# A hybrid encoder layer on one core: a third PSUM bank for main products, heads' norms by square transposes, and two moved ScalarE/VectorE steps

## The chip, the cores and the metric

The kernel runs on one core of a Trainium2 chip. The metric is the time of one execution on the device in microseconds (us). Five engines work side by side, each on its own instructions in a fixed order, and wait for one another by semaphores: TensorE (PE in the profile, its weight loads PEld), VectorE (DVE), ScalarE (ACT), GpSimd (POOL) and SyncE (SP, which here issues most of the DMAs). TensorE writes its results to PSUM, which has eight banks of 128 x 512 float32 here; the other data lies in SBUF.

## The reference

One layer of an encoder, batch 1, 512 tokens, width 1024, in float32. The part that the change touches is the parallel mixer:

```python
h = _rms_norm(x, norm_mix_pre)
(a_q, a_k, a_v, f_q, f_k, f_v, f_g, c_u, s_x, s_b, s_c) = split(h @ w_in)
# A, differential attention, 4 heads, keys up to the query's chunk of 64:
p = softmax(where(chunk mask, s * scale, -inf))          # two score maps per head
ya = (p[0] - lam * p[1]) @ v
ya = _rms_norm(ya, diff_norm) * (1 - lambda_init)        # over the 128 channels of a head
# B, forgetting attention, 8 heads, causal, bias from a cumulative log forget gate:
yf = softmax(where(causal, s * scale + c_q - c_k, -inf)) @ v
# C, gated convolution of 31 taps with a LayerNorm; D, gated convolution of 3 taps
proj = einsum(stack([ya, yf, yc, ys]), w_branch)
mixed = sum(sigmoid(h @ w_gate + b_gate) * proj) @ w_out
x = x + _rms_norm(mixed, norm_mix_post)
```

Behind it come a cross-attention into 256 memory tokens and a gated MLP with a convolution of 3 taps; the change leaves their code alone.

## The kernel before

Every large product is made of three: each operand is split into a high part (a cast to fp32r, by ScalarE) and a low part (the rest, a subtraction by VectorE), and high x high, high x low and low x high are summed in one PSUM bank (`mm3`). Weights come from HBM as blocks of 512 KB into one of two raw tiles `wr`, are cast to `wh` (L192) and subtracted to `wl` (L193), of which there are four each.

The work is a list of jobs (`run_blocks`). A job's weights are fetched three jobs ahead; its body is usually a product of 128 channels by 512 tokens over eight pieces of 128 rows, so 24 matmuls of 512 columns (`channel_major`), and then its evacuation from PSUM. Beside the jobs run background tasks (`Background`): generators that yield a cost and a waiting time after each step. At each tick, in the middle and at the end of a job, they get credit (0.7 per us of products counted so far, at most 4), and the first two in the queue may take steps as long as credit is left. `drain` runs what is left of a kind at once. This sets the program's order; a scheduler at build time then orders each engine's instructions from it, by dependences, free buffers and its own estimate of times, and `tc.issue_after(x)` places an instruction behind `x` on its engine.

PSUM's eight banks have four names with two banks each: `mm` and `av` (main products; `av` also for the attentions' values), `sc` (scores) and `tr` (transposes). `bank()` without a name takes `mm` and `av` in turn, and only `mm` between `share(False)` and `share(True)`, the two attention stages, where `av` holds values.

The jobs around the change: values of A (`v_jobs`); four pairs of query and key products of A (`qk_jobs`), each of which adds a background task for a head (`a_task`, heads 0 to 3), among them the 12 jobs of gate and branch for the convolution (`gate_blocks(2, "c")`); drain of A's tasks; the values of B (`vf_jobs`, four jobs, whose result takes the one tile `v` that held A's values); four pairs of query and key products of B, each of which adds `f_task` (pairs of heads 0 to 3), among them gate and branch of A; drain of B's tasks; gate and branch of B; then the layer's other parts.

A head of A works in steps, one per 128 queries: scores (two per step, `sc`), exponentials, the difference of the two maps. Heads 0 to 2 ("far") have their probabilities turned to keys-major form by VectorE's square transposes of 32 x 32 blocks (`turn_squares`) and a way through DRAM (`put`, `get`), and split in place two steps later (`split_in_place`); head 3 has them turned on TensorE (`to_keys_major`). Pairs 0 and 1 of B are far, 2 and 3 near. The values of two steps are then summed into an `av` bank (`values`). Head A's end, from L949 on, is its RMS norm: the 128 x 512 result is turned to token-major form by four TensorE transposes, squared (L953), summed (L955), its root taken by GpSimd, scaled (L957), turned back by four more transposes and split into `y["a"]`. The LayerNorm of the convolution (`conv_norm_task`) does the like without TensorE's transposes: VectorE transposes squares of 32 x 32, sums over 32 columns, and one small product with a constant (`over_channels`, L871) adds the four blocks of channels.

`evacuations` holds the newest evacuation that was marked by `main`, `last_weights` the newest weight block's cast and subtraction. In `f_task` the two heads' probabilities are scaled by ScalarE (L1135, `j` = 0) and VectorE (L1133, `j` = 1).

Of the kernel before, what the change touches and what calls it, by code (L numbers as in the profile page):

```python
# [83 lines left out]
def hybrid_layer(ctx: ExitStack, tc: tile.TileContext, a: dict, out: bass.AP):  # L84
# [9 lines left out]

    turn_of = SimpleNamespace(n=0, shared=True)

    def bank(tag=None):
        if tag is None:
            turn_of.n += 1
            tag = "av" if turn_of.shared and turn_of.n % 2 else "mm"  # L100
        return psum.tile([P, 512], F32, tag=tag, name=f"ps_{tag}", bufs=2)

    def share(shared):
        return None, None, lambda: vars(turn_of).update(n=1, shared=shared)

# [755 lines left out]

    def split_in_place(n, pt, local):
        hi, lo = (part_of(x, n, local) for x in pt)
        raw = lo.bitcast(F32)
        with tc.issue_after(evacuations[0]):
            A.copy(hi, raw)
        V.tensor_tensor(lo, raw, hi.bitcast(F32), ALU.subtract)
# [27 lines left out]
    def a_task(h, qk, v):  # L895
# [3 lines left out]
        for step in range(8 if far else 6):  # L899
# [8 lines left out]
            if far:  # L908
                for qt in SPLITS.get(step, ()):
                    split_in_place(qt + 1, pt, qt % 2)  # L910
                    cost += 0.1 + 0.15 * qt
                for qt in GETS.get(step, ()):
                    if qt % 2 == 0:
                        pt = pt_tiles()
                    get(es.pop(qt)[:, 0], qt + 1, pt, qt % 2)
            elif 1 <= step <= 4:
                if step in (1, 3):
                    pt = pt_tiles()
                to_keys_major(es.pop(step - 1)[:, 0], step, pt, (step - 1) % 2)
                cost += 0.1 + 0.15 * step  # L920
# [27 lines left out]
            yield cost, (6.0 if step == 5 else 4.0) if far else 3.5  # L948

        ps = bank("tr")  # L950
        for t in range(NT):
            transpose(ps[:, t * P:(t + 1) * P], e[:, 0, t * P:(t + 1) * P])
        A.activation(e[:, 1], ps, AF.Square, scale=1.0 / math.sqrt(P))  # L953
        ms = m1p.tile([P, NT], F32, tag="ms4", name="ms4", bufs=2)
        V.tensor_reduce(ms, e[:, 1].rearrange("p (t c) -> p t c", t=NT), AX.X, ALU.add)  # L955
        r = rstd_of(m1p, [ms], NT)
        V.tensor_tensor(e[:, 0].rearrange("p (t c) -> p t c", t=NT),  # L957
                        ps.rearrange("p (t c) -> p t c", t=NT),
                        r.unsqueeze(2).to_broadcast([P, NT, P]), ALU.mult)
        yield 1.5, 3.5  # L960
        ps2 = bank("tr")
        for t in range(NT):
            transpose(ps2[:, t * P:(t + 1) * P], e[:, 0, t * P:(t + 1) * P])
        if "a" not in y:
            y["a"] = (y8b(), y8b())
        split(ps2, y["a"][0][:, h], y["a"][1][:, h], half["dn"])
        yield 0.6, 0.0

# [85 lines left out]
    def f_task(p, qk, v):  # L1054
# [19 lines left out]
        for step in range(8 if far else 6):  # L1074
# [14 lines left out]
            if far:  # L1089
# [4 lines left out]
                for qt in GETS.get(step, ()):  # L1094
# [3 lines left out]
                    for j in range(2):  # L1098
                        get(d[:, j], qt + 1, pts[j], qt % 2)
            else:  # L1100
                for qt in {2: (0, 1), 3: (2,), 4: (3,)}.get(step, ()):
                    if qt % 2 == 0:
# [5 lines left out]
            if step < 4:  # L1108
# [22 lines left out]
                for j in range(2):  # L1131
                    if j:
                        V.tensor_scalar(e[:, j, :w], e[:, j, :w], st[:, 6 + j:7 + j], None, ALU.mult)  # L1133
                    else:
                        A.activation(e[:, j, :w], e[:, j, :w], AF.Copy, scale=st[:, 6 + j:7 + j])  # L1135
# [59 lines left out]
    def mixer_jobs():  # L1195
# [20 lines left out]
        yield from vj  # L1216
        yield share(False)
        gc = gate_blocks(2, "c")
# [121 lines left out]
    def last_branch_jobs():  # L1340
# [3 lines left out]
        yield next(gf)  # L1344
        yield share(True)
        yield from gf
# [544 lines left out]
```

## Time and profile before

| | |
|---|---|
| median of 3 runs | 1051.34 us (1051.13 to 1052.14) |
| profiled execution | 1050.01 us, its span 1048.2 us, TensorE's granted clock 0.999 |
| busy, of the span | TensorE 1037.6, weight loads 882.5, VectorE 807.9, ScalarE 508.5, GpSimd 147.5 us |
| first transposes of a head's norm on TensorE | 279.18 us after the start; attention A's queue is empty at about 359 us |
| far pairs of attention B | about 380 to 440 us |

In the profile, a row of a group gives line, engine, operation, the tiles written and read, their shapes and the count; then busy time and the mean length in ns, and the idle time of the engine before them with what ended it. Rows of the timeline give start and length in us. Matmul lengths contain the pipeline's depth, so that two matmuls overlap; how far apart they start tells what one costs. In a row of waits stand the engine, tile and line that waited, what it waited for, the sum in us, the number of times and the longest.

### The profile page before, as it was taken

How to read it: one execution, taken by the hardware profiler on the slowest of the kernel's cores; microseconds unless marked ns; L12 is line 12 of the kernel's file. 1: busy time of each engine (PE TensorE's matmuls, PEld its weight loads, DVE VectorE, ACT ScalarE, POOL GpSimd, SP SyncE). 2: the span in 40 equal slices, each digit the busy share in tenths (PEclk: the TensorE clock that was granted, in tenths of full speed). 3: DMA queues.
4: the chain of work that ended last, by engine and by line, in shares of the span. 5: the costliest groups of instructions: out<-in, count | busy, mean ns of one | idle time of the engine just before them, and what ended most of it. 6: DMA issues, size and time to landing. Idle time of an engine off the chain costs nothing.

```text
span 1048.2 us, 14451 instructions
## 1 busy us (share of the span) xinstructions
PE 1037.6 (99%) x5255; PEld 882.5 (84%) x5255; DVE 807.9 (77%) x1265; ACT 508.5 (49%) x838; POOL 147.5 (14%) x239
## 2 busy tenths in 40 slices
PE   8999999999999999999999999999999999999997
PEld 8888888888888988888888899998888888888886
DVE  7999998677768369876577898776767777667796
ACT  5322222376465356765443666655343333445662
POOL 4001000100000114432101031121112111111001
PEclk9999999999999999999999999999999999999999
DMA  8953333334433246642357734235577666726662
GB/s 272 315 158 90 102 100 101 99 85 122 137 103 110 61 122 186 181 136 81 101 160 265 237 124 137 63 104 189 191 241 225 217 224 218 220 81 183 215 215 81
DMA packets 182141, 163.86 MB, mean 156 GB/s; under 512 B 17151, under 2 KB 154092, under 8 KB 182069
## 3 DMA queue, kind: packets, MB, share of 16 engines
q1 hardware_dynamic: 173027, 131.18, 42.0%
q10 hardware_dynamic: 6482, 23.21, 6.2%
q0 software_dynamic: 2560, 8.54, 2.5%
q8 instruction: 41, 0.67, 0.3%
q14 instruction: 31, 0.25, 0.1%
HBM read 139.43 MB, written 23.48 MB: 155 GB/s over the span
## 4 chain that ended last, share of the span: by engine, by line
PE 98%; DVE 1%; DMA 0%; ACT 0%; issue 0%; POOL 0%; POOLq 0%; DVEq 0%; SPq 0%; ACTq 0%
PE ps_mm L235 53%; PE ps_av L235 30%; PE ps_sc L235 7%; PE ps_tr L235 4%; PE ps_tr L241 2%; PE ps_mm L453 1%; PE ps_av L453 1%; DMA xs<-in_x 0%; ACT e L735 0%; DVE qk L808 0%; PE ps_tr L437 0%; DVE o L1781 0%; PE ps_av L437 0%; ACT qk L806 0%; DVE e L848 0%
## 5 line engine op out<-in xcount | busy, mean ns | idle before, releaser
L192 ACT CAST wh<-wr 128x1024 fp32r<-128x1024 f32 (+1 forms) x140 | 146.6, 1048 | 261.5 <-PE ps_mm L235 158.2
L193 DVE TENSOR_TENSOR wl<-wr,wh 128x1024 fp32r<-128x1024 f32 (+1 forms) x140 | 174.7, 1249 | 85.5 <-ACT wh L192 85.3
L235 PE MATMUL ps_mm<-hth,wh 128*128 128x512 f32 (+1 forms) x616 | 230.5, 381 | 0.4 <-DVE qk L808 0.2
L235 PE MATMUL ps_mm<-hth,wl 128*128 128x512 f32 (+1 forms) x616 | 229.8, 379 | 0.0
L235 PE MATMUL ps_mm<-htl,wh 128*128 128x512 f32 (+1 forms) x616 | 229.7, 379 | 0.0
L235 PEld LDWEIGHTS ps_mm<-hth,wh 128*128 128x128 f32 x616 | 114.1, 188 | 21.9 <-ACT y L158 0.6
L235 PEld LDWEIGHTS ps_mm<-hth,wl 128*128 128x128 f32 x616 | 114.0, 188 | 21.4
L235 PEld LDWEIGHTS ps_mm<-htl,wh 128*128 128x128 f32 x616 | 114.0, 188 | 20.5
L235 PE MATMUL ps_av<-htl,wh 128*128 128x512 f32 (+1 forms) x328 | 122.5, 373 | 0.0
L235 PE MATMUL ps_av<-hth,wh 128*128 128x512 f32 (+1 forms) x328 | 122.4, 373 | 0.0
L235 PE MATMUL ps_av<-hth,wl 128*128 128x512 f32 (+1 forms) x328 | 122.3, 373 | 0.0
L688 DVE SCALAR_TENSOR_TENSOR y<-y,par,y 128x508 f32<-128x508 f32 (+29 forms) x120 | 82.9, 731 | 0.1
L235 PEld LDWEIGHTS ps_av<-hth,wl 128*128 128x128 f32 x328 | 61.7, 188 | 11.0
L235 PEld LDWEIGHTS ps_av<-htl,wh 128*128 128x128 f32 x328 | 61.6, 188 | 10.9
L235 PEld LDWEIGHTS ps_av<-hth,wh 128*128 128x128 f32 x328 | 61.6, 188 | 10.8
L1682 DVE TENSOR_TENSOR wl<-dw,wh 128x1024 fp32r<-128x1024 f32 x32 | 40.1, 1257 | 15.6 <-ACT wh L1681 15.4
L1681 ACT CAST wh<-dw 128x1024 fp32r<-128x1024 f32 x32 | 33.5, 1052 | 22.0 <-PE ps_mm L235 7.4
L1629 ACT ACTIVATE th<-c 128x512 f32<-128x512 f32 x22 | 13.9, 632 | 48.1 <-DVE c L615 48.1
L1116 POOL TENSOR_SCALAR fbias<-ck,cq 128x128 f32<-128x128 f32 (+3 forms) x32 | 27.0, 847 | 70.4 <-DVE st L1122 63.2
L615 DVE SCALAR_TENSOR_TENSOR c<-ps_mm,par,c 128x510 f32<-128x510 f32 (+1 forms) x44 | 32.8, 745 | 0.7
L235 PE MATMUL ps_mm<-y8b,wh 128*128 128x512 f32 x96 | 30.7, 396 | 0.0
L235 PE MATMUL ps_mm<-y,wh 128*128 128x512 f32 x96 | 30.6, 393 | 0.0
(484 smaller groups left out, 2092.4 us busy)
## 6 DMA issues: line engine op xcount, KB each, us to landing
wr<-in_w_up SPq DMA_DIRECT2D x44, 512.0 KB
wr<-in_w_in SPq DMA_DIRECT2D x38, 512.0 KB
wr<-in_w_gate SPq DMA_DIRECT2D x32, 512.0 KB
wp<-in_w_down ACTq DMA_DIRECT2D x22, 512.0 KB
sums<-wp ACTq DMA_DIRECT2D x22, 512.0 KB
dw<-sums SPq DMA_DIRECT2D x44, 256.0 KB
wr<-in_w_branch SPq DMA_DIRECT2D x16, 512.0 KB
wide<-in_w_out SPq DMA_DIRECT2D x12, 512.0 KB
```

Of the source, the lines that this page charges most:

```text
L192: last_weights[:] = [order(A.copy(hi, raw[:, :n])).ins, low.tensor_tensor(lo, raw[:, :n], hi.bitcast(F32), ALU.subtract).ins]
L193: low.tensor_tensor(lo, raw[:, :n], hi.bitcast(F32), ALU.subtract).ins]
L235: steps_of[:] = [PE.matmul(ps, lhs, rhs, start=start, stop=stop).ins]
L241: turns.append(PE.transpose(ps, x, ident[:n, :n]).ins)
L453: keep(PE.matmul(banks[c][:, :S // 2], w[p == 1][:, k, c * P:(c + 1) * P], ht[p == 2][:, i * 4 + k, :S // 2], start=(i, p, k) == (0, 0, 0) ...
L615: ins = V.scalar_tensor_tensor(dst[:, s:], src[:, :S - s], w(k), dst[:, s:], ALU.mult, ALU.add)
L688: ins = V.scalar_tensor_tensor(dst[:, s:], src[:, :S - s], pc("conv_dw", k * 4 + j), dst[:, s:], ALU.mult, ALU.add)
L1116: G.tensor_scalar(bias[:, :w], ck[j][:, :w], -1.0, cq[:, qt, head:head + 1], ALU.mult, ALU.add)
L1629: A.activation(th, c[:, 0], AF.Silu)
L1681: A.copy(hi, x)
L1682: V.tensor_tensor(lo, x, hi.bitcast(F32), ALU.subtract)
```

## The change

- `bank` gets a list of names among which main products take turns. In the attention stages it is `mm`, `mm`, `tr0`: the two `tr` banks become `tr0` and `tr1`, and as long as `tr0` is in the list, transposes take `tr1` alone. From the second step of pair 2 of B on (`step == 2 and p == 2`) the list is `mm`, and transposes have both again; from the last gate stage on it is `mm`, `av` as before.
- The norm of a head of A: one square transpose of the whole result by VectorE, the squares by ScalarE, a sum over 32 columns, `over_channels`, the power by GpSimd on 128 x 16, the scaling, a square transpose back, the split. TensorE's eight transposes per head go, one small product comes. The costs told to `Background` are 2.0, 0.2 and 2.4 with waits of 4.0 and 4.0, in place of 1.5 and 0.6 with a wait of 3.5.
- `split_in_place` takes what its cast is placed behind; in `a_task` it is now `last_weights`. `f_task` still passes nothing and keeps `evacuations`.
- In the far pairs of `f_task` both heads' probabilities are scaled by VectorE.

```diff
--- before.py
+++ after.py
@@ -92,16 +92,22 @@
 
 
 
-    turn_of = SimpleNamespace(n=0, shared=True)
+    turn_of = SimpleNamespace(n=0, tr=0, among=("mm", "av"))
 
     def bank(tag=None):
         if tag is None:
             turn_of.n += 1
-            tag = "av" if turn_of.shared and turn_of.n % 2 else "mm"
-        return psum.tile([P, 512], F32, tag=tag, name=f"ps_{tag}", bufs=2)
-
-    def share(shared):
-        return None, None, lambda: vars(turn_of).update(n=1, shared=shared)
+            tag = turn_of.among[turn_of.n % len(turn_of.among)]
+        elif tag == "tr":
+            turn_of.tr = 1 if "tr0" in turn_of.among else 1 - turn_of.tr
+            tag = f"tr{turn_of.tr}"
+        return psum.tile([P, 512], F32, tag=tag, name=f"ps_{tag}", bufs=1 if tag[:2] == "tr" else 2)
+
+    def share_now(*among):
+        vars(turn_of).update(n=1, among=among)
+
+    def share(*among):
+        return None, None, lambda: share_now(*among)
 
     x_d, mem_d = a["x"][0], a["mem"][0]
     w_in, w_gate, w_out = a["w_in"][0], a["w_gate"][0], a["w_out"][0]
@@ -859,10 +865,10 @@
     def get(d, n, pt, local):
         SP.dma_start(part_of(pt[1], n, local).bitcast(F32), d.rearrange("(a j) (b x) -> (j b) a x", j=32, b=4))
 
-    def split_in_place(n, pt, local):
+    def split_in_place(n, pt, local, after=evacuations):
         hi, lo = (part_of(x, n, local) for x in pt)
         raw = lo.bitcast(F32)
-        with tc.issue_after(evacuations[0]):
+        with tc.issue_after(after[0]):
             A.copy(hi, raw)
         V.tensor_tensor(lo, raw, hi.bitcast(F32), ALU.subtract)
 
@@ -907,7 +913,7 @@
             cost = 0.0
             if far:
                 for qt in SPLITS.get(step, ()):
-                    split_in_place(qt + 1, pt, qt % 2)
+                    split_in_place(qt + 1, pt, qt % 2, last_weights)
                     cost += 0.1 + 0.15 * qt
                 for qt in GETS.get(step, ()):
                     if qt % 2 == 0:
@@ -947,24 +953,22 @@
                 A.copy(e[:, 0], av)
             yield cost, (6.0 if step == 5 else 4.0) if far else 3.5
 
+        V.transpose(e[:, 1], e[:, 0])
+        A.activation(e[:, 0], e[:, 1], AF.Square, scale=1.0 / math.sqrt(P))
+        ms = m1p.tile([P, S // 32], F32, tag="ms4", name="ms4")
+        V.tensor_reduce(ms, by_token(e[:, 0]), AX.X, ALU.add)
+        yield 2.0, 4.0
         ps = bank("tr")
-        for t in range(NT):
-            transpose(ps[:, t * P:(t + 1) * P], e[:, 0, t * P:(t + 1) * P])
-        A.activation(e[:, 1], ps, AF.Square, scale=1.0 / math.sqrt(P))
-        ms = m1p.tile([P, NT], F32, tag="ms4", name="ms4", bufs=2)
-        V.tensor_reduce(ms, e[:, 1].rearrange("p (t c) -> p t c", t=NT), AX.X, ALU.add)
-        r = rstd_of(m1p, [ms], NT)
-        V.tensor_tensor(e[:, 0].rearrange("p (t c) -> p t c", t=NT),
-                        ps.rearrange("p (t c) -> p t c", t=NT),
-                        r.unsqueeze(2).to_broadcast([P, NT, P]), ALU.mult)
-        yield 1.5, 3.5
-        ps2 = bank("tr")
-        for t in range(NT):
-            transpose(ps2[:, t * P:(t + 1) * P], e[:, 0, t * P:(t + 1) * P])
+        over_channels(ps[:, :S // 32], ms)
+        V.tensor_scalar(ms, ps[:, :S // 32], EPS, None, ALU.add)
+        G.tensor_tensor(ms, ms, nhalf[:, :1].to_broadcast([P, S // 32]), ALU.pow)
+        yield 0.2, 4.0
+        V.tensor_tensor(by_token(e[:, 1]), by_token(e[:, 1]), ms.unsqueeze(2).to_broadcast([P, S // 32, 32]), ALU.mult)
+        V.transpose(e[:, 0], e[:, 1])
         if "a" not in y:
             y["a"] = (y8b(), y8b())
-        split(ps2, y["a"][0][:, h], y["a"][1][:, h], half["dn"])
-        yield 0.6, 0.0
+        split(e[:, 0], y["a"][0][:, h], y["a"][1][:, h], half["dn"])
+        yield 2.4, 0.0
 
 
     crows = dram.tile([8, S], F32, name="crows")
@@ -1098,6 +1102,8 @@
                     for j in range(2):
                         get(d[:, j], qt + 1, pts[j], qt % 2)
             else:
+                if step == 2 and p == 2:
+                    share_now("mm")
                 for qt in {2: (0, 1), 3: (2,), 4: (3,)}.get(step, ()):
                     if qt % 2 == 0:
                         pts = [pt_tiles() for _ in range(2)]
@@ -1129,7 +1135,7 @@
                                  scale=HD ** -0.5, accum_out=st[:, 4 + j:5 + j])
                 V.reciprocal(st[:, 6:8], st[:, 4:6])
                 for j in range(2):
-                    if j:
+                    if j or far:
                         V.tensor_scalar(e[:, j, :w], e[:, j, :w], st[:, 6 + j:7 + j], None, ALU.mult)
                     else:
                         A.activation(e[:, j, :w], e[:, j, :w], AF.Copy, scale=st[:, 6 + j:7 + j])
@@ -1214,7 +1220,7 @@
             yield then(lambda f=f, q=q: f(q))
             yield then(lambda q=q: out_sums.store(q))
         yield from vj
-        yield share(False)
+        yield share("mm", "mm", "tr0")
         gc = gate_blocks(2, "c")
         for h, n in enumerate((0, 2, 4, 6)):
             yield from qk_jobs(O_AQ, O_AK, h, lambda qk, h=h: bg.add(a_task(h, qk, va), "a"))
@@ -1342,7 +1348,7 @@
         gf = gate_blocks(1, "f", mix_place, mix_done)
         yield next(gf)
         yield next(gf)
-        yield share(True)
+        yield share("mm", "av")
         yield from gf
```

## The prediction

> **What bounds the kernel now.** I read the page first, then the waits with TensorE as the waiting engine, then windows of 20 us, and last the timeline around the steps that the diff touches. From the page, the span, the engines' busy shares and the chain that ended last:
>
> ```profile
> span 1048.2 us, 14451 instructions
> PE 1037.6 (99%) x5255; PEld 882.5 (84%) x5255; DVE 807.9 (77%) x1265; ACT 508.5 (49%) x838; POOL 147.5 (14%) x239
> PE 98%; DVE 1%; DMA 0%; ACT 0%; issue 0%; POOL 0%; POOLq 0%; DVEq 0%; SPq 0%; ACTq 0%
> ```
>
> The chain is TensorE (PE) from end to end. The waits with PE as the waiting engine are only these four (total us, times, longest):
>
> ```profile
> PE ps_tr L437 <- DVE nt L432: 1.4, 1, 1.4
> PE ps_mm L394 <- DVE e L344: 1.3, 1, 1.3
> PE ps_mm L235 <- DVE qk L808: 0.2, 1, 0.2
> PE ps_tr L241 <- ACT e L947: 0.2, 1, 0.2
> ```
>
> The first two lie in the first 10 us, which the diff leaves alone. In the attention stages PE idles 0.4 us in all. So TensorE gains from work that leaves it, hardly from waits. The other engines there (window, its length, then busy us and instructions of PE, PEld, DVE, ACT, POOL, granted clock, DMA share, GB/s):
>
> ```profile
> 340.00:360.00 20.00, 19.79 (x168) 19.55 (x166) 7.38 (x16) 5.79 (x12) 2.88 (x5) 1.00 0.11 28
> 400.00:420.00 20.00, 20.00 (x98) 16.71 (x97) 18.50 (x45) 11.14 (x25) 8.42 (x18) 1.00 0.76 218
> 420.00:440.00 20.00, 20.00 (x99) 16.94 (x98) 16.50 (x34) 16.51 (x35) 7.44 (x15) 1.00 0.64 176
> ```
>
> VectorE is at 18.5 of 20 us just where the far pairs of the forgetting attention run (400 to 440), and nearly empty at 340 to 360, where attention A's queue is emptied. Both matter below.
>
> **The norm of the four heads.** Before, each head has two groups of four transposes on TensorE, 32 in all; after, one small product (`over_channels`) per head and two square transposes on VectorE. One group of four, and the nearest row of the small product, which the convolution's norm already uses at L871 (start, length, instruction):
>
> ```profile
> 288.29 0.60 PE L241 MATMUL ps_tr<-ident,e 128*128 128x128 f32 x4
> 288.65 0.48 PE L235 MATMUL ps_mm<-hth,wl 128*128 128x512 f32 x1
> 288.96 0.39 PE L235 MATMUL ps_mm<-hth,wh 128*128 128x512 f32 x1
> ...
> 186.00 0.29 PE L871 MATMUL ps_tr<-bn,across 128*128 128x16 f32 x2
> 186.14 0.48 PE L235 MATMUL ps_mm<-y8b,wh 128*128 128x512 f32 x1
> 186.45 0.39 PE L235 MATMUL ps_mm<-y8b,wl 128*128 128x512 f32 x1
> ```
>
> Lengths of PE rows overlap, so I go by starts. The usual step from one 512-wide product to the next is 5.44/24 = 0.23 us, by this row of the chain in order of time (start, length, count):
>
> ```profile
> 40.41 5.44 PE ps_mm L235 x24
> ```
>
> A group of four transposes takes 288.65 - 288.29 = 0.36 us, and the product behind it 0.31 (to 288.96) in place of 0.23, so 0.44 where it stands alone. Eight groups are 2.9 us; the 0.08 counts for some six of them, since at the queue's end they run together: 3.4 us removed. The small product takes 0.14 and again 0.08 behind it: 4 x 0.22 = 0.9 us added. Net 2.5 us less on PE, all of it on the path, because PE does not wait.
>
> VectorE pays for it:
>
> ```profile
> L727 DVE STREAM_TRANSPOSE xn<-y 128x512 f32<-128x512 f32 x4 | 2.7, 696 | 0.0
> L705 DVE TENSOR_SCALAR bn<-ps_tr 128x16 f32<-128x16 f32 x2 | 0.3, 175 | 1.5 <-PE ps_tr L871 1.5
> L1133 DVE TENSOR_SCALAR e<-e,st 128x512 f32<-128x512 f32 x4 | 1.9, 485 | 0.1
> L1135 ACT ACTIVATE e<-e,st 128x512 f32<-128x512 f32 x4 | 2.9, 722 | 0.9 <-DVE st L1130 0.9
> ```
>
> Per head 2 x 0.70 + 0.18 = 1.6 us more (square, sum, scaling and split stay), 6.3 us in some 130 us: covered by its idle time. Without that cover it would delay a weight's low part, which PE needs only two jobs later.
>
> **Far pairs scaled by VectorE.** Eight instructions (two pairs, four widths) move from ScalarE (0.72 us at 512 wide) to VectorE (0.49 at that width). VectorE gets at most 8 x 0.49 = 3.9 us, mostly in the window where it has 1.5 us free; ScalarE is relieved by more. PE waits for none of these now; I take 0, with bounds of 0 and +3.9.
>
> **Cast behind weights.** In attention A `split_in_place`'s cast on ScalarE is ordered behind the newest weight cast (L192) instead of the newest evacuation. No DMA moves with it; the low part on VectorE follows it. What it may wait for now, and a second row used later:
>
> ```profile
> ACT wh L192 <- PE ps_mm L235: 158.9, 60, 4.7
> ...
> DVE e L1122 <- POOL fbias L1118: 4.9, 2, 4.3
> ```
>
> A weight cast waits for PE to free a buffer, 158.9/60 = 2.6 us on average, 4.7 at most. Behind it on ScalarE now stands the turned cast, then VectorE's low part, and for them wait the products with the values, which the code puts at least 4 us of products later. So I take 0. The bounds: six such steps (three far heads, two each), each late by 4.7 - 4.0 = 0.7 us, are +4.2 us, and far off, since PE frees that buffer as a job begins and the steps are taken at its middle or end; below zero it cannot go, as PE has no wait on these casts to lose.
>
> **Third bank.** What it can remove is a main product waiting for a bank. There are two such places:
>
> ```profile
> 220.06 0.39 PE L235 MATMUL ps_mm<-hth,wl 128*128 128x512 f32 x1
> 220.68 0.47 PE L235 MATMUL ps_mm<-hth,wh 128*128 128x512 f32 x1 [0.23 <-DVE qk L808]
> ...
> 441.17 0.39 PE L235 MATMUL ps_mm<-y8b,wl 128*128 128x512 f32 x1
> 441.69 0.50 PE L235 MATMUL ps_mm<-hth,wh 128*128 128x512 f32 x1
> ```
>
> The first stretch is 0.62 us, the second 0.52, where 0.23 is usual: 0.7 us, less the slower refill that a new bank's group may keep: I take 0.6 off, bounds 0 and 0.7. The transposes lose one of their two banks while this holds; what that costs is in the next part.
>
> **The queue of attention A at its end.** This is the one place where the diff can lose much. Background steps are paid for with credit, 0.7 per us of products, at most 4. The old norm costs 1.5 + 0.6 = 2.1, the new one 2.0 + 0.2 + 2.4 = 4.6, and waits 8 us in place of 3.5. Heads 0 and 1 go through it while heads 2 and 3 stand behind them: 2 x 2.5/0.7 = 7 us of products later, somewhat more than one job of 5.44. I walked the queue through with the code's costs. Before, after the last branch product of the convolution (`body_b`, which ends at 336.44 + 0.23) there is left: head 2's second half of the values, head 3's third set of transposes and first half of values, and at the drain two norms and head 3's last step. The trace has just that order. After, there remain besides: head 2's first half of values and its last turned tiles, and head 3's scores at 384 and 512 wide. Before, the row of the last scores stands 4 us ahead of that end:
>
> ```profile
> 332.32 1.09 PE L235 MATMUL ps_sc<-qk 128*128 128x512 f32 x4
> 336.44 0.40 PE L235 MATMUL ps_mm<-y,wl 128*128 128x512 f32 x1
> 339.03 0.33 PE L235 MATMUL ps_mm<-wh,hth 128*128 128x256 f32 x1
> 341.53 0.75 DVE L938 SCALAR_TENSOR_TENSOR e<-e,st 128x512 f32<-128x512 f32 x1 [0.85 <-ACT e L937]
> 345.05 1.04 PE L241 MATMUL ps_tr<-ident,e 128*128 128x128 f32 x8
> 348.56 0.28 PE L235 MATMUL ps_av<-pth,v 128*128 128x256 f32 x1
> 349.92 0.62 PE L241 MATMUL ps_tr<-ident,e 128*128 128x128 f32 x4
> 351.17 0.37 PE L235 MATMUL ps_av<-wh,hth 128*128 128x264 f32 x1
> ```
>
> And the split of a set of transposes, from the groups by form:
>
> ```profile
> L155 ACT CAST pth<-ps_tr 128x512 fp32r<-128x512 f32 x5 | 2.8, 583 | 4.7 <-PE ps_tr L241 4.6
> L156 DVE TENSOR_TENSOR ptl<-ps_tr,pth 128x512 fp32r<-128x512 f32 x5 | 3.3, 689 | 4.4 <-ACT pth L155 4.4
> ```
>
> What covers the chain from scores to values is the next job's products (`vf_jobs`, first seen at 339.03). Two tokens of them need four banks, one of which head 3's values hold, and their result goes into the tile `v` (one buffer) that those values still read: three groups of 24 can run, no more. From 339.03 to 348.56 less the eight transposes at 345.05 (two groups, 0.7) that is 8.8 us. After the change PE has besides, up to the last values: the same 2.4 us as before (from 336.67 to 339.03), another first half of values (half of 349.92 - 348.56) 0.7, two transposes 0.2, scores 512 wide 4 x 0.23 = 0.9 and 384 wide 0.7, four transposes 0.4; 5.3 us, with 8.8 makes 14.1. The chain: from the scores (332.32) to the probabilities (341.53 + 0.75) it took 10.0 us; transposes 0.36, cast 0.58 and low part 0.69 make 11.6 to the values. The scores at 512 wide need the banks that those at 384 have just filled: values 0.7, transposes 0.2, the scores themselves 0.7 and twice 0.69 until VectorE has read them, so they start 3.0 us after that branch product. Values are ready at 14.6, and PE starves for 14.6 - 14.1 = 0.5 us. Bounds: 0, if the chain runs faster with VectorE as empty as at 340 to 360; and, if scores to values take the 348.56 - 332.32 = 16.2 us of before, 3.0 + 16.2 - 14.1 = 5.1. I take 0.5: the probabilities stood ready 2.8 us (342.28 to 345.05) before PE's order took them up, so the 16.2 hold slack. With one transpose bank in place of two, two sets follow one another by a split of 1.3 us, inside these bounds.
>
> **Sum.** -2.5 - 0.6 + 0.5 = -2.6 us. The profiled execution took 1050.01 us (span 1048.2 and 1.8 around it), so 1047.4 after; the median of the three runs is 1051.34 (1051.13 to 1052.14), 1.3 above it, so **1048.7 us** as a median. About 0.2% (2.1 us) is what a measurement of this kernel can tell from no change.
>
> **Rivals.** (1) *The change does not do what it says.* The bank removes no wait, and the drained queue takes back what the transposes gave, 2 to 3 us: -2.5 + 2.5 = 0, 1051.3, no change. For it: the transposes at 345.05 stood 2.8 us behind their data: PE's order was drawn up for a slower chain than the real one; if it is so again, the transposes come after all three groups, and their split (0.58 + 0.69) lies open. Against: PE waited 0.2 us there.
> (2) *Slower: the drained queue starves PE.* One mechanism at one place, 335 to 355 us: head 3's last scores come after the last branch product, and the three groups run out before its values are ready. At the upper bound, 5.1, and with nothing gained by the bank: -2.5 + 5.1 = +2.6, so 1053.9. It decides from 2.5 + 2.1 = 4.6 us of starving on. For it: the 16.2 us of before; against: much of those was waiting in PE's order. No row here shows PE's clock after such a gap. By the Trainium skill (TensorE: Matmul & The Clock Gate, Part 1: The HAM clock gate) an idle window of some 3.4 us halves the clock for as long again; an estimate by that rule makes this rival some 1.7 us longer (half of 3.4 lost), 1055.6.
> (3) *VectorE and GpSimd bind in the far pairs.* With 18.5 of 20 us busy, 3.9 us more do not fit; scores then keep their banks and PE waits for what exceeds the 1.5 us free: 2.4, so -2.6 + 2.4 = -0.2, 1051.1. For it: VectorE already waited 4.9 us for GpSimd's bias (the L1122 row). Against: the windows beside it have 3.5 us free. The Trainium skill (SBUF — State Buffer, Who interferes with whom) says that a `tensor_scalar` may take the port pair it shares with GpSimd, which then fully blocks; the moved scaling is that kind, and by that rule the bias would come late by up to the whole 3.9 us, an estimate of 1052.6. No row before shows GpSimd held up so.
>
> **Chances.** Forecast 0.60, of which 0.44 beyond 2.1 us (the drain costs under 1.0 us) and 0.16 within it; rival 1 0.16, all within; rival 2 0.18, all slower; rival 3 0.06, 0.02 within and 0.04 slower when the full 3.9 comes with some of rival 1. Faster 0.44, same 0.34, slower 0.22. The range goes from 1047.4 (-2.5 - 0.7 and no cost at the drain is -3.2, so 1048.1, less 0.7 for the spread of the runs) to 1053.9, rival 2's place.
>
> **What would show it.** 32 transposes fewer under `ps_tr<-ident,e` (50 of 82), eight more rows of the small product (two each), two square transposes per head on VectorE, L1135 8 times in place of 16; no PE gap at some 220 and 440 us; `ps_tr` products in the attention stages that are main products. At the drain, the time from the last branch product to the first product behind head 3's values: 351.17 - 336.44 = 14.7 us before, and for the forecast a PE idle sum under 1.5 us there. Over 4 us would be rival 2; VectorE over 19.5 of 20 us at 400 to 420 with PE waits on `ps_sc` rival 3. Waits of PE on turned casts (`pth`, `ptl`) would prove the cast's 0 wrong.

## The result and the profile after

The changed kernel takes 1058.32 us (1056.39 to 1060.99, four runs), the kernel before on the same chip 1051.51: a ratio of 1.0063 (95% interval 1.005 to 1.0075), some 6.8 us slower. The forecast was 1048.7, the range ended at 1053.9.

The page of the changed kernel's profile, span, busy times and the chain that ended last:

```profile
span 1059.2 us, 14416 instructions
PE 1042.5 (98%) x5231; PEld 884.7 (84%) x5231; DVE 817.0 (77%) x1285; ACT 505.3 (48%) x830; POOL 152.1 (14%) x235
PE 55%; DMA 2%; DVE 1%; ACT 1%; issue 1%; POOL 0%; POOLq 0%; DVEq 0%; SPq 0%; ACTq 0%
```

TensorE has 24 instructions fewer (32 transposes gone, 8 small products new) and is yet busy 4.9 us longer; the chain no longer is TensorE's from end to end. The waits with PE as the waiting engine (us in total, times, longest; most lines are numbered 6 higher than before):

```profile
PE ps_sc L241 <- DVE st L1128: 3.0, 2, 2.2
PE ps_mm L241 <- ACT ge L1170: 1.8, 1, 1.8
...
PE ps_av L241 <- ACT pth L161: 0.7, 1, 0.7
...
PE ps_av L241 <- ACT e L953: 0.5, 1, 0.5
PE ps_tr L247 <- DVE e L944: 0.5, 1, 0.5
PE ps_av L241 <- DVE ptl L162: 0.3, 1, 0.3
```

None of these six rows has a counterpart before. (Left out are two waits of the program's first 10 us, and one of 0.2 us in attention B for a turned cast at L872.) The norm's steps, by groups of one form:

```profile
L247 PE MATMUL ps_tr<-ident,e 128*128 128x128 f32 x50 | 8.2, 274 | 0.5 <-DVE e L944 0.5
L877 PE MATMUL ps_tr<-ms,across 128*128 128x16 f32 x8 | 1.2, 227 | 0.0
L964 POOL TENSOR_TENSOR ms<-ms,nhalf 128x16 f32<-128x16 f32 x4 | 11.6, 2896 | 34.5 <-DVE ms L963 34.5
L1141 ACT ACTIVATE e<-e,st 128x512 f32<-128x512 f32 x2 | 1.5, 727 | 0.4 <-DVE st L1136 0.4
```

50 transposes of 82 are left, eight small products are new, ScalarE scales 2 times at this width in place of 4: the change does what it says.

To find the place of the loss, I took for each matmul of TensorE the time to the start of the next, less what its form usually takes (0.227 us for 512 columns, 0.118 for 256, 0.109 for a transpose of 128), and summed this excess by stages, from 180 us on; "drain" goes from the convolution's last branch product (332 us) to the end of the values' products of B (367 us), "B" from there to the last product of B with values (531.7 us):

| us beyond the usual steps | attention A | drain | B | rest of the program |
|---|---|---|---|---|
| before | 2.1 | 0.8 | 3.0 | -0.1 |
| after | 1.4 | 5.3 | 12.0 | 0.5 |

The sum rises by 13.4 us, while the last product starts 10.7 us later (1051.4 in place of 1040.7): some 2.7 us of work did go, as worked out, and 4.5 at the drain and 9.0 in B came in its place. That is this execution; it is the slowest of the four, for a reason that its windows show (third number from the end: granted clock; second: DMA share):

```profile
345.00:350.00 5.00, 3.53 (x27) 2.91 (x26) 2.22 (x4) 1.33 (x3) 0.51 (x1) 1.00 0.00 0
350.00:355.00 5.00, 4.50 (x25) 4.40 (x25) 3.15 (x8) 2.00 (x5) 2.89 (x1) 0.66 0.02 3
...
415.00:420.00 5.00, 2.78 (x16) 2.21 (x15) 4.36 (x8) 0.57 (x1) 0.57 (x2) 0.91 0.33 96
420.00:425.00 5.00, 5.00 (x17) 3.94 (x17) 3.98 (x8) 2.95 (x7) 1.66 (x3) 0.75 0.62 167
...
476.00:481.00 5.00, 3.17 (x13) 2.25 (x13) 3.80 (x8) 4.16 (x10) 2.02 (x5) 0.95 0.42 105
481.00:486.00 5.00, 5.00 (x18) 3.98 (x18) 3.98 (x11) 1.58 (x4) 1.69 (x4) 0.70 0.38 108
```

Behind each of three stretches in which TensorE idled 1.5 to 2.2 us, its clock falls: 5 x 0.34 = 1.7 us of clock lost at 350, 0.45 + 1.25 = 1.7 at 415 to 425, 0.25 + 1.5 = 1.75 at 476 to 486. These 5.2 us lie in the 17.3 of drain and B. The four runs differ in the same way: 1056.39 and 1057.08 us at a mean clock of 0.998, 1059.55 at 0.995, 1060.99 at 0.993. So a gap costs its own length and, in some executions, 1.7 us more.

### The profile page after: what moved, and what is told of

Same layout as the page of the kernel before. It is cut to its first block, busy times and chain, and to the rows that moved or that the text cites. A ratio compares the mean times of both kernels' runs of the same rounds, so it can differ in the third digit from the quotient of the medians.

```text
span 1059.2 us, 14416 instructions
## 1 busy us (share of the span) xinstructions
PE 1042.5 (98%) x5231; PEld 884.7 (84%) x5231; DVE 817.0 (77%) x1285; ACT 505.3 (48%) x830; POOL 152.1 (14%) x235
## 4 chain that ended last, share of the span: by engine, by line
PE 55%; DMA 2%; DVE 1%; ACT 1%; issue 1%; POOL 0%; POOLq 0%; DVEq 0%; SPq 0%; ACTq 0%
PE ps_mm L241 25%; PE ps_av L241 19%; PE ps_sc L241 6%; PE ps_tr L241 4%; PE ps_tr L247 1%; DMA turned<-e 1%; DMA ptl<-turned 1%; ACT e L1134 0%; DVE wl L199 0%; DVE e L854 0%; ACT wh L198 0%; DVE e L1128 0%; ACT ge L1170 0%; DVE e L1153 0%; DVE e L1139 0%
## 5 line engine op out<-in xcount | busy, mean ns | idle before, releaser
L241 PE MATMUL ps_mm<-hth,wh 128*128 128x512 f32 (+1 forms) x544 | 201.8, 378 | 0.0
L241 PE MATMUL ps_mm<-htl,wh 128*128 128x512 f32 (+1 forms) x544 | 201.5, 378 | 0.0
L241 PE MATMUL ps_mm<-hth,wl 128*128 128x512 f32 (+1 forms) x544 | 201.3, 377 | 0.0
L241 PEld LDWEIGHTS ps_mm<-hth,wh 128*128 128x128 f32 x544 | 100.6, 188 | 18.5 <-ACT hth L161 0.3
L241 PEld LDWEIGHTS ps_mm<-hth,wl 128*128 128x128 f32 x544 | 100.5, 188 | 18.4
L241 PEld LDWEIGHTS ps_mm<-htl,wh 128*128 128x128 f32 x544 | 100.6, 188 | 18.1
L241 PEld LDWEIGHTS ps_av<-htl,wh 128*128 128x128 f32 x328 | 61.5, 188 | 10.8
L1122 POOL TENSOR_SCALAR fbias<-ck,cq 128x128 f32<-128x128 f32 (+3 forms) x32 | 24.5, 768 | 81.1 <-DVE st L1128 62.3
L241 PE MATMUL ps_sc<-qk 128*128 128x128 f32 (+3 forms) x128 | 28.9, 321 | 3.0 <-DVE st L1128 3.0
L621 DVE SCALAR_TENSOR_TENSOR c<-ps_av,par,c 128x510 f32<-128x510 f32 (+1 forms) x40 | 29.8, 746 | 0.6
```

The costliest lines, as they stand in the source:

```text
L241: steps_of[:] = [PE.matmul(ps, lhs, rhs, start=start, stop=stop).ins]
L621: ins = V.scalar_tensor_tensor(dst[:, s:], src[:, :S - s], w(k), dst[:, s:], ALU.mult, ALU.add)
L1122: G.tensor_scalar(bias[:, :w], ck[j][:, :w], -1.0, cq[:, qt, head:head + 1], ALU.mult, ALU.add)
```

## The experiments

Ratios are to the kernel before on the same chip, with 95% intervals. The figures for the drain and B come from one profiled execution of each kernel, which can lie some 2 us from the median (the changed kernel's 2.7 above it, that of the kernel before 1.5 below), so differences of 1 us between them carry little. Two theories stood at first: the *queue* (the norm's longer costs and waits leave attention A's tail without cover), and *VectorE in B* (the moved scaling, rival 3 of the prediction).

**Each part undone by itself.** Scaling back to ScalarE:

```diff
-                    if j or far:
+                    if j:
```

> The changed kernel, but the far pairs' first head is scaled by ScalarE again. Theory V (the scaling loads VectorE, so scores keep their banks and TensorE waits in the far pairs of attention B): the 9.5 us that the stretch from the last vf product to the end of B grew by go, 1058.3 comes down to about 1049. Theory B (the third bank, with one bank left for transposes, makes an order of TensorE's instructions that the other engines cannot follow): no change, 1056 to 1060. The wait at attention A's end (some 4 us) stays under both.

Measured: 1055.56 us, 1.0039 (1.0023 to 1.0055). Drain 3.9, B 7.6. The third bank taken out (`bank` and `share` as before):

> The changed kernel, but main products take mm alone in the attention stages and transposes have both tr banks. Theory B: the far pairs' loss goes, about 1049, and with two banks for transposes also part of the wait at attention A's end. Theory V: 1056 to 1060, the waits on scores stay.

Measured: 1054.59 us, 1.003 (1.0018 to 1.0043). Drain 1.8, B 6.2. So without the third bank, too, the other parts cost some 3 us; the largest waits of this kernel, at 441.8 and 367.6 us, are these:

```profile
PE ps_mm L235 <- ACT ge L1162: 1.7, 1, 1.7
PE ps_mm L235 <- DVE v L156: 1.6, 1, 1.6
```

The heads' norm as before, with its eight transposes per head:

> The changed kernel, but with the old norm (eight transposes per head on TensorE, old costs). Theory D (the new norm's credit delays heads 2 and 3, so TensorE starves where attention A's queue is emptied): the waits between the first and the last vf product fall from 5.3 to under 1 us while TensorE gets 2.5 us of work back, so 2 us faster there; under V and B the far pairs' 9.5 us stay, about 1056. If the far pairs' loss comes from what the norm moves, about 1048.

Measured: 1051.42 us, 1.0002 (0.9992 to 1.0012). Drain 1.3, B 3.2: the loss is gone, and with it the gain. The cast back behind the evacuation:

```diff
-                    split_in_place(qt + 1, pt, qt % 2, last_weights)
+                    split_in_place(qt + 1, pt, qt % 2)
```

> The changed kernel, but the turned tiles of attention A are cast behind evacuations again. All theories: no change beyond the runs' own spread, 1056 to 1060. A fall of over 3 us would show that the cast's place matters.

Measured: 1059.27 us, 1.0073 (1.0057 to 1.009). The new place is not what costs; the old one has a gap of 1.0 us at 341.7 before head products with values, which the new one lacks.

The loss needs the norm, but undoing the bank or the scaling takes part of it as well. No part alone makes up the sum.

**The queue by itself.** The norm as changed, but `Background` is told neither costs nor waits:

```diff
-        yield 2.0, 4.0
+        yield 0.0, 0.0
...
-        yield 0.2, 4.0
+        yield 0.0, 0.0
...
-        yield 2.4, 0.0
+        yield 0.0, 0.0
```

> The changed kernel, but the new norm tells Background no cost and no wait (0.0, 0.0 at its three yields), the same instructions otherwise. Theory Q (the norm holds one of the queue's two places longer, so heads 2 and 3 are late when the queue is drained, and what is late there makes attention B's start late): by the walk through the code's costs only the two norms are left at the drain, the waits between the first and the last vf product fall from 5.3 to under 1.5 us, those up to the end of B from 12 to under 5, and the time is 1047 to 1051. Theory N (the new norm's own chain on VectorE and GpSimd is what is late): 1056 to 1060 as before.

Measured: 1055.45 us, 1.0039 (1.0027 to 1.0051), 4 us above what the queue theory allowed. Drain 1.8 in place of 5.3. The timeline of this kernel, PE at the place where the changed one starved, has two waits left, both for the bank of values to be copied out:

```profile
343.37 0.62 PE L247 MATMUL ps_tr<-ident,e 128*128 128x128 f32 x4
344.21 0.39 PE L241 MATMUL ps_av<-wh,hth 128*128 128x264 f32 x1 [0.22 <-ACT e L953]
...
347.00 0.28 PE L241 MATMUL ps_av<-pth,v 128*128 128x256 f32 x1
...
349.44 0.39 PE L241 MATMUL ps_av<-wh,hth 128*128 128x264 f32 x1 [0.50 <-ACT e L953]
```

The values at 347.00 wait for nothing. So the told costs are needed for the drain's loss. They are not enough for it: with the same costs and two banks for transposes (the run without the third bank, and the norm alone below) the three waits that stand ahead of the values in the changed kernel are missing as well. B still loses 9.1. With ScalarE's scaling too:

> As told_nothing, and the far pairs' first head scaled by ScalarE again. Theory Q with V (VectorE's extra scaling hurts only where attention B is already late): no different from told_nothing by more than 1.5 us. If the scaling costs 2.8 us by itself, as taking it back from the changed kernel gave, 2 to 3 us faster than told_nothing.

Measured: 1055.55 us, 1.0042 (1.0026 to 1.0059). Drain 1.8, B 8.1. Here the scaling makes no difference, so VectorE in B falls as a cause of its own.

**One part alone.** Only the norm, then only the bank, on the kernel before:

> The kernel before with the new norm alone, its costs as in the change. Theory Q: TensorE has 2.5 us less to do, the drain costs 1 to 2 us, attention B starts late by as much: 1051 to 1055. If the norm is harmless by itself and only the combination hurts: 1048.8.

Measured: 1050.71 us, 0.9993 (0.9984 to 1.0003); B 4.7.

> The kernel before with the third bank alone (transposes have one bank while it holds). If the bank takes away the two waits of main products and costs nothing: 1050.7. If one bank for transposes is what starves TensorE at attention A's end (4 us between first and last vf product): 1054 or more.

Measured: 1050.38 us, 0.9992 (0.9982 to 1.0001); B 2.5. Each is at or a little under the time before. The norm alone gives 0.8 us, not the 2.5 of TensorE's work that it takes away: its drain and its B lose more than before, with a wait of 1.2 us where the values' products of B end. Hence the next question: do the two suffice together, and is it the bank in attention B?

> Norm and third bank, without the VectorE scaling and with the cast in its old place. Theory C (the loss in attention B needs the new norm and the third bank, and only these): TensorE's steps in the last branch's stage lose 7 to 8 us as in the full change with ScalarE's scaling (7.6), the drain 4 to 5, 1055 to 1056 us. Rival S (each part only reshuffles the order, and the loss of the full change is a chance meeting of all four): the stage loses under 5, and the time is under 1053.

Measured: 1058.75 us, 1.0072 (1.0057 to 1.0087). Drain 5.2, B 10.8: norm and bank alone are enough for a loss as large as the full one. The number missed the expectation by 3 us, two half-clock stretches among them. This kernel and the one with the scaling undone (1055.56) differ in the cast's place alone, so the new place saved some 3 us here; one of the waits that it takes away is 1.0 us long, at 341.9 us, for a turned cast of attention A.

**The bank given back.** In the kernel told nothing, with ScalarE's scaling, one line behind A's drain:

```diff
         yield then(lambda: bg.drain("a"))
+        yield share("mm")
```

> The change with the planner told nothing of the norm's waits and with ScalarE's scaling, and the third bank given back when attention A's queue has been drained. Theory C1 (the bank itself hurts while attention B runs: the main products that run ahead on three banks are what B's products and evictions then stand behind): the stage's loss falls from 8.1 to the 3 to 5 us of the kernels without the bank, the drain stays at 1.8, 1050 to 1051.5 us. Rival C2 (attention B pays for what attention A left behind, its start and the queues of VectorE and ScalarE, and not for the bank): the stage still loses 7 to 9, 1054.5 to 1056.

Measured: 1051.49 us, 1.0003 (0.9993 to 1.0012). B falls from 8.1 to 5.6; 1.9 of what is left is a new wait where the values' products end. Its row in the waits of this kernel:

```profile
PE ps_mm L241 <- DVE v L162: 1.7, 1, 1.7
```

> The new norm alone, the planner told nothing of its waits. Theory Q (the norm's told waits hold a place of the background queue; without them attention A's queue is empty earlier): the drain loses under 1.5 instead of 1.8, the stage of attention B 3 to 5 as with the norm alone (4.7), 1048.5 to 1050.5 us. Rival (with two transposes' banks the drain was never short, and steps come out of order instead): 1050.5 to 1052, stalls on the values' casts inside attention A.

Measured: 1051.04 us, 1.0002 (0.9993 to 1.0012). Drain 0.7, but the same new wait at 365 us (2.0), so nothing is won: the time went from one place to its neighbour. The same with the cast behind the weights:

> The new norm and the cast behind the weights, the planner told nothing, no third bank, ScalarE's scaling. Theory C: without the bank attention B loses 3 to 5, the drain under 2, 1049 to 1051 us; against the kernel with the bank (1055.5) that is 4 to 6 us less. Rival S: anything else in attention B, above 6, and 1053 or more.

Measured: 1052.66 us, 1.0009 (1.0 to 1.0019). Drain 0.7, the same wait (2.1). Its time lies 1.7 us above what was expected. It is also 1.6 us above the kernel just shown, which differs in the cast's place alone; its profile has a gap of 0.8 us at 263.0 us that the other lacks.

The same one line in the change as it was made, so with its queue and its scaling:

> The change as made, with the third bank given back to the transposes once attention A's queue has been drained. Theory C1 (the bank held while attention B runs is what costs there): the last branch's stage loses 4 to 7 us instead of 12, the drain stays at 5.3, no stretch at half clock near 419 or 480, 1052 to 1055 us. Rival C2 (B pays for what A left behind and for the scaling on VectorE): the stage loses 9 or more, 1057 to 1059 us.

Measured: 1053.25 us, 1.0018 (1.0008 to 1.0027): 5 us less than the change. Drain 3.9, B 5.9. The bank only from A's drain on:

> New norm, told nothing, ScalarE's scaling, the cast behind the weights; the third bank only from the drain of attention A's queue on, the transposes' two banks before. Theory C1: the stage loses 7 to 9 us as with the bank throughout (8.1), 1054 to 1056 us, the drain under 1. Rival C3 (A's single bank of transposes, by the order in which it leaves A's work, is needed for the loss): the stage loses under 6, 1050 to 1052.5 us.

Measured: 1052.46 us, 1.0007 (0.9996 to 1.0018). B 4.7, as the rival had it, though a gap of 2.0 us in front of a gate product is there (471.8 us). So bank and norm in B are enough for that gap. That the rest of B's loss needs attention A's single bank of transposes as well, by what it leaves behind, is likely and not shown: the profiled execution, 1050.45 us, is the fastest of ten that reach 1055.9. The bank kept for one job more, until the wait at 366 us is past, and then given back:

```diff
         yield from kv_blocks(0)
+        yield share("mm")
```

> As the kernel that gives the bank back after the drain, but given back only behind the first key and value block. If the wait of 1.9 us at 366 us for VectorE's split of the values is the price of two banks at that place, it is gone, the stage loses 3 to 4.5 us and the time is 1049 to 1050.5 us. Rival (the order of attention B's work is settled by what is issued there, so the bank must be gone before): the stage loses 6 or more, 1052 to 1055 us.

Measured: **1049.15 us**, 0.9975 (0.9966 to 0.9984), faster than both kernels. Drain 1.8, B 3.5; neither the gap at the values' end nor the one before the gate product is there. The same line with the bank alone, old norm:

> The third bank alone, without the new norm, given back behind the first key and value block. Theory C1 in its strict form (the bank in attention B costs by itself): 1 to 2 us less than with the bank held throughout (1050.4), 1048.5 to 1049.5 us. Theory C (norm and bank have to meet): 1050 to 1051 us, the stage's loss at 2 to 3.5 us as before.

Measured: 1051.92 us, 1.0005 (0.9995 to 1.0014), B 3.3: above both expectations, and no better than with the bank held throughout (1050.38). So the bank in B costs nothing where the norm is the old one: the two have to meet.

**The change with its two faults taken out,** all else as made, its scaling on VectorE too (three yields of zero, and the line above):

> The change as made (its scaling on VectorE, its cast, its norm) with two edits: the planner told nothing of the norm's waits, and the third bank given back behind the first key and value block. Theory T (the two causes are the whole loss, and the scaling only made their stalls longer): 1048.5 to 1050.5 us, within 1 us of the kernel that also has ScalarE's scaling (1049.15), last branch's stage losing 3 to 4.5 us. Rival V (VectorE's six longer scalings cost attention B by themselves, as rival 3 of the prediction had it): 1051 to 1053 us, the stage losing 5.5 or more, with waits on VectorE's reduces of the scores.

Measured: **1049.12 us**, 0.998 (0.9971 to 0.9989). Drain 1.8, B 3.7. Its page, busy times and chain:

```profile
PE 1036.4 (99%) x5231; PEld 880.8 (84%) x5231; DVE 816.5 (78%) x1285; ACT 504.0 (48%) x830; POOL 156.6 (15%) x235
PE 97%; DVE 1%; DMA 1%; ACT 1%; issue 0%; SPq 0%; POOL 0%; POOLq 0%; DVEq 0%; ACTq 0%
```

TensorE is its own chain again, with 1.2 us less busy time than before.

**How the bank costs in B.** In the waits of ScalarE one row tells whether the bank is held there: the wait for the end of a pair of heads, which VectorE adds up (`y<-e` behind L1153; L1145, L1147 or L1155 in other kernels). Of the changed kernel, of the bank alone, of the norm alone, and of the kernel of 1049.15 us:

```profile
ACT y L161 <- DVE e L1153: 4.8, 4, 2.7
```

```profile
ACT y L161 <- DVE e L1155: 3.7, 3, 1.9
```

```profile
ACT y L155 <- DVE e L1145: 0.7, 1, 0.7
```

```profile
ACT y L161 <- DVE e L1153: 0.7, 1, 0.7
```

In all nine kernels that hold the bank while B's pairs run, the longest is 1.9 to 2.7 us; in the ten that do not, before among them, 0.7 to 0.8. ScalarE works in a fixed order, so all behind that wait is late. The row marks the bank and not yet the loss, since with the bank alone it is 1.9 us long and nothing is lost. What norm and bank make together is a gap of 2.0 us in front of a gate product, between 471.8 and 480.4 us: it is there in all seven kernels that hold the bank in B and have the new norm, and in neither of the two that hold it with the old one. (The kernel without the third bank has one of 1.8 us at another gate product, at 441.8.) The timeline of the changed kernel where it hits TensorE:

```profile
472.61 1.39 DVE L824 TENSOR_TENSOR qk<-ps_mm,qk 64x512 fp32r<-64x512 f32 x2 [1.68 <-ACT qk L822]
...
475.39 1.39 DVE L1153 TENSOR_TENSOR e<-ps_av,e 64x512 f32<-64x512 f32 x2
...
476.81 0.62 ACT L161 CAST y<-e 128x512 fp32r<-128x512 f32 x1 [2.69 <-DVE e L1153]
...
479.61 0.69 ACT L1170 ACTIVATE ge<-ps_mm,s_b_gate 128x512 f32<-128x512 f32 x1
480.35 1.07 PE L241 MATMUL ps_mm<-y8b,wh 128*128 128x512 f32 x2 [1.82 <-ACT ge L1170]
```

VectorE's q/k subtraction waits for ScalarE, the pair's end comes behind it, ScalarE waits 2.69 us for that, and the gate's tanh, which alone empties the bank that TensorE wants, stands behind two exponentials and a weight cast. The other large gap, at 419 us, is of the same sort: ScalarE waits 2.41 us for a turned tile on its way through DRAM, VectorE waits for ScalarE's cast, then works without a pause from 413.66 on, and its reduce of scores, which frees the bank that TensorE wants, has its turn only at 418.50:

```profile
411.67 0.41 ACT L872 CAST pth<-ptl 128x256 fp32r<-128x256 f32 x1 [2.41 <-DMA ptl<-turned]
412.10 0.43 DVE L873 TENSOR_TENSOR ptl<-ptl,pth 128x256 fp32r<-128x256 f32 x1 [2.13 <-ACT pth L872]
...
418.50 0.68 DVE L1128 CUSTOM_DVE_ANT_0 e<-ps_sc,fbias 128x512 f32<-128x512 f32 x1
...
419.24 0.69 PE L241 MATMUL ps_sc<-qk 128*128 128x128 f32 x2 [2.22 <-DVE st L1128]
```

What stays open is why a longer wait of ScalarE reaches TensorE only with the new norm (1.9 us of ScalarE's waiting, and no gap over 1 us on TensorE, with the bank alone). Each edit changes the order of all engines' instructions, and no run isolates which order is needed.

## Why the prediction was wrong

The gain was worked out rightly, the loss was not: the drain was set at +0.5 us and measured +4.5, and the waits of TensorE in attention B, which the sum took at nothing, cost 9.0 more than before, the slower clock behind them included. Term by term:

- **The norm's transposes, -3.4 + 0.9: right.** The counts are as foretold, and the steps' sums leave some 2.7 us of work gone.
- **The third bank, -0.6: right at its place, wrong beyond it.** The wait at 220 us is gone, and attention A loses 1.4 in place of 2.1. That more room for products could make an eviction late was not in any step, and the one bank left for transposes was taken to stay "inside these bounds".
- **The drain, +0.5: the term that was mis-sized; it measured +4.5.** What is left in the queue was walked through rightly: head 3's scores at 384 and 512 wide do come behind the last branch product. Its timeline in the changed kernel:

```profile
331.93 0.40 PE L241 MATMUL ps_mm<-y,wl 128*128 128x512 f32 x1
...
338.07 0.63 PE L241 MATMUL ps_sc<-qk 128*128 128x512 f32 x2
...
346.68 0.63 PE L247 MATMUL ps_tr<-ident,e 128*128 128x128 f32 x4 [0.45 <-DVE e L944]
347.98 0.39 PE L241 MATMUL ps_av<-pth,v 128*128 128x256 f32 x1 [0.68 <-ACT pth L161]
348.71 0.39 PE L241 MATMUL ps_av<-ptl,v 128*128 128x256 f32 x1 [0.34 <-DVE ptl L162]
...
350.89 0.59 PE L241 MATMUL ps_av<-wh,hth 128*128 128x264 f32 x1 [0.50 <-ACT e L953]
351.28 0.42 PE L241 MATMUL ps_av<-wl,hth 128*128 128x264 f32 x1
```

The 512 wide scores start 5.9 us after that product (338.07 - 332.16), where 3.0 had been set; from there to the values it takes 9.9, where 11.6 had been. So the values are ready at 15.8, not 14.6, and TensorE starts late by 0.6 + 0.8. Then come two waits that the step left out: for the low part behind the high part (0.6), and for the copy of the values out of their bank (0.7). Last comes the clock, 1.7 us: from 351.28 on products of 264 columns start 0.22 us apart in place of 0.12. Rival 2 had the mechanism, the place and the clock; its starving was set at 5.1 us and measured 2.8, the four waits together, with the clock's 1.7 behind them. The starving needs two parts: the costs and waits told to the queue, since the run told nothing lacks it (drain 1.8), and the single bank for transposes, since the run without the third bank lacks it with the costs as told (1.8). There head 3's 512 wide scores start 1.2 us after the end of the last branch product (335.03), in one run and not in two halves:

```profile
336.21 1.09 PE L235 MATMUL ps_sc<-qk 128*128 128x512 f32 x4
```

The step gave the single bank no price of its own.
- **PE waits in B stay at nothing: the step that failed without having been written.** The sum took the state before, 0.4 us of idling, as given ("So TensorE gains from work that leaves it, hardly from waits"), and the diff's parts one by one. B's 9.0 us are two thirds of the excess that this execution gained, and most of them come from two parts, norm and bank, whose kernels alone are no slower than before: giving the bank back takes 5 us off the changed kernel (1053.25).
- **Far scaling 0: right for the scaling by itself.** 1049.12 with it on VectorE (0.998 of the time before on its chip), 1049.15 without (0.9975). In the full change undoing it took 2.8 us. Why is open: a starved drain is not enough for it, since with the cast in its old place and the drain just as starved the kernels with the scaling on VectorE and on ScalarE took 1059.27 and 1058.75. Rival 3 had its wait on `ps_sc` but the wrong cause: VectorE is not full there (and at 16.46 of 20 us from 420 to 440). The window of the changed kernel, VectorE's 12.96 us of 20 behind PE and PEld:

```profile
400.00:420.00 20.00, 17.78 (x83) 14.65 (x82) 12.96 (x33) 6.98 (x16) 6.22 (x14) 0.98 0.50 137
```

That a scaling of this kind may block GpSimd (the Trainium skill, SBUF — State Buffer, Who interferes with whom) shows in no run as a cost. VectorE's wait for GpSimd's bias, with the scaling on VectorE, and with it on ScalarE (the two fastest kernels):

```profile
DVE e L1128 <- POOL fbias L1124: 4.7, 3, 3.9
```

```profile
DVE e L1128 <- POOL fbias L1124: 4.6, 2, 4.0
```

Before it was 4.9, in the changed kernel 5.6.
- **The cast 0: not what made the loss, but not 0 either.** The waits on casts that are left in the changed kernel are for head 3's transposes (`pth`, L161) and for one turned cast of B (0.2 us, L872); the edit touches neither. "Below zero it cannot go" held for the kernel before alone: with the new norm and the bank the old place brings a wait of 0.9 to 1.0 us at 342, and with the scaling on ScalarE it is 3.2 us slower (1058.75 against 1055.56). With the scaling on VectorE the two places do not differ clearly (1059.27 against 1058.32), and without the bank and with nothing told the new one's median is 1.6 us higher (1052.66 against 1051.04).

With the two faults taken out the change gives -2.1 us (1049.12 against 1051.22), near the sum of -2.6. That is no proof of the sum: it had neither edit in it, and it was made for the kernel that lost 6.8 us.

## What to carry to other kernels

On an engine that is busy to 99%, work taken away is worth its time only if each other engine's order still gives back banks in time; the price of a cheap edit was here a gap of 1 to 2 us at some other place, and at times as much again for the clock. Parts that cost nothing alone can cost much together, so they are to be tried in pairs too. Room for running ahead (a bank more) is to be held only where a wait shows that it is wanted: here until the first key and value block, not through the next attention. Where a cost told to a planner decides what is left at a drain, try it at zero before judging the edit by its time; for the norm without the bank that gained nothing (1051.04 against 1050.71), so it is a trial and no rule.

## What the runs showed of the hardware

A gap of 2.39 us at 419 us in TensorE's products was followed by products 0.43 us apart in place of 0.227 until 422.4, and four gaps of 0.6 to 0.8 us within 5 us (346 to 351) did the same. Others had no such effect. A low clock came behind the gap of 2.0 us before a gate product in the profiles of three kernels (the changed one, with 0.70 from 481 to 486 us, the one with the cast undone, and norm and bank alone); seven others have a gap of 1.9 to 2.05 us, there or where B's values' products end, and a full clock behind it. In the kernel told nothing with ScalarE's scaling this gap ends at 474.6, and the granted clock stays full by its windows:

```profile
474.00:476.00 2.00, 1.44 (x6) 1.22 (x7) 2.00 (x4) 1.55 (x4) 0.00 (x0) 1.00 0.18 72
476.00:481.00 5.00, 5.00 (x30) 4.36 (x30) 4.93 (x12) 2.70 (x6) 1.69 (x4) 1.00 0.36 108
```

The Trainium skill (TensorE: Matmul & The Clock Gate, Part 1: The HAM clock gate) names, in its table of states, an idle window of some 3.4 us as the condition. The loss of 1.7 us per case agrees with half of that window; the condition does not, since shorter gaps were enough, in some executions and not in others. The power on GpSimd takes 2.9 us for 128 x 16 (L964), and stands in the norm's chain once per head.
